# Softmax denominators on 64 rows per head, a division in quarters, and an earlier place for the first output tile

## The chip, the core and the metric

The kernel runs on one core of one Trainium2 chip. The metric is the device time of one execution in microseconds (us), lower is better. Of the core's engines, PE (TensorE) multiplies matrices, with PEld for its weight loads; DVE (VectorE), ACT (ScalarE) and POOL (GpSimd) work on elements; SP (SyncE) issues the DMAs.

## The reference

One inference step of a trunk of two layers, over 1024 latent tokens ("sample") and 128 context tokens ("prompt"), width 1024, all in fp32. Layer 0 joins grouped-query attention (mixer A, 8 heads of 64, 1152 keys for a latent token) with a pooling mixer B; layer 1 joins a neighbourhood attention (mixer C) with a latent attention (mixer D, 8 heads, keys of 96, values of 64). The change touches the softmax of A and D and the output projections behind them:

```python
def blocked_attention(q, k, v):
    ...
        s = jnp.einsum('bqkgd,bnkd->bkgqn', qblk, k, preferred_element_type=jnp.float32) * scale
        p = jax.nn.softmax(s, axis=-1).astype(v.dtype)
        return jnp.einsum('bkgqn,bnkd->bqkgd', p, v)
...
    y = jnp.concatenate([o_a * jax.nn.silu(ga), o_b * jax.nn.silu(gb)], axis=-1) @ w_out
```

## The kernel before, in words

The order of instructions on each engine is the order in which the Python code issues them; semaphores, put in by the framework, make an engine wait for its inputs and for free buffers. `weave(main, fill, frac)` (L27) spreads the steps of `fill` evenly over the first `frac` of the steps of `main`, by the costs written beside each step.

A and D each run as eight **units**, one for a pair of heads and half of the latent tokens (512). A unit goes over nine key tiles of 128 keys (`kt` 0 to 8, called the first to the ninth). For each key tile and head, PE makes scores `st` [128 keys, 512 queries] in PSUM, and ACT takes the exponential into `P` (or `Px`). For the denominator, POOL adds the `P` of the key tiles into `acc` [128, 2 heads, 512]; in the last unit of a mixer DVE does it. PE multiplies `P` with the values into one PSUM bank `pv`, which has 64 rows for each head, in the groups of key tiles of `PV_GROUPS`: 0 and 1 behind key tile 3, 2 and 3 behind 5, 4 to 6 behind 8, and 7 and 8 inside the next unit. Between these, the next unit's maxima are made as `fill`: 24 times PE forms a piece of scores `mp` [128 queries, 384 keys] and DVE reduces it (`mx`, L948), then `ms` (L953) joins them and PE turns them into a row (`mT`), which the next unit's scores subtract.

The **end of a unit** runs as a list `tail` within the next unit, one step per key tile: the last `pv`; nothing; gate times `pv` into `gT()` (a slice of `oT` in A, of `gd` in D); then `ColSums`. Its `sums` (fourth key tile) has PE sum `acc` over the keys with a matrix of ones, four matmuls of 32 rows by 256 queries, into a bank `sum`, and DVE takes half of the reciprocals. `split` (fifth) takes the other half and splits the result `srow` in two parts that PE can read without loss, `Rhl`: the high one by a cast on ACT, the low one by a subtraction on DVE. `spread` (seventh) has PE copy these rows to the 64 rows of each head (bank `rb`, four matmuls with the constant `oneh`), and DVE multiplies `gT()` with it. The context tokens' attention in A (`prompt_A`, woven into units 3 to 5 as `side` steps, with `mpp`, `msp`, `mTp`) uses `ColSums` as well; that of D makes its sums pair by pair (`dsum`), has ACT copy them to a tile `psum`, and normalises all of them in `prompt_norm` at the end.

PSUM has eight banks of [128, 512]: three for `st` (tag A), five taken in turn by everything else (tag B: `mp`, `pv`, `sum`, `rb`, `mT`, `ggp` and the rest).

Behind the units comes the output projection `outproj` (L1213). For each of nine token tiles it splits the branch outputs into two parts `ohl` (a cast on DVE, a subtraction on POOL), PE multiplies them with the weights `whi` and `wlo` (the split of `raw`, by ACT and POOL) into two banks `yps`, and `post` normalises. Its first steps, `pre` (the gate rows `ggp`, two loads, the splits of tile 0), are `fill` of the last unit, spread over the first 77% of its steps (after a placeholder of cost 18000 in layer 0, in `extra`). The last unit's own tail runs inside the first output tile.

Of the kernel before, what the change touches and what calls it, by code (L numbers as in the profile page):

```python
# [55 lines left out]
class Kern:  # L56
# [108 lines left out]
    def setup(self):  # L165
# [13 lines left out]
        self.oneh = self.K([128, 2, 128], F32R, name="oneh")  # L179

    def setup2(self):
        oh = self.W([128, 2, 128], name="oh0")
        self.dma(oh, self.I["k_oneh"])
        self.vcopy(self.oneh, oh)
        self.negid = self.K([128, 128], F32R, name="negid")
        self.vts(self.negid, self.ident, -1.0)
# [742 lines left out]
class Unit:  # L929
# [71 lines left out]

    def fin(self):

        kn = self.kn
        R = ColSums(kn)

        def f0():
            g = self.gT()
            kn.vtt(g, g, self.pv)
        return [(1, f0), (440, lambda: R.sums(lambda h, c: self.acc[:, h, 256 * c:256 * c + 256])), (1, R.split),  # L1010
                (1, lambda: None), (440, lambda: R.spread(self.gT()))]


class ColSums:


    def __init__(self, kn):
        self.kn = kn

    def sums(self, src):  # L1020
        kn = self.kn
        b = self.b = kn.B("sum")[:, 0:256]
        for h in range(2):
            for c in range(2):
                o = 64 * h + 32 * c
                kn.mm(b[o:o + 32], kn.ones, src(h, c))
        self.R = kn.T([128, 256], tag="srow", bufs=1)
        self.half(0)

    def half(self, i):  # L1030
        c = slice(128 * i, 128 * i + 128)
        self.kn.nc.vector.reciprocal(out=self.R[:, c], in_=self.b[:, c])  # L1032

    def split(self):
        kn = self.kn
        self.half(1)
        hl = self.hl = kn.T([128, 2, 256], F32R, tag="Rhl", bufs=1)
        kn.acopy(hl[:, 0], self.R)
        kn.vtt(hl[:, 1], self.R, f32(hl[:, 0]), ALU.subtract)

    def spread(self, g):

        kn, hl = self.kn, self.hl
        b = kn.B("rb")
        for c in range(2):
            for x in range(2):
                kn.mm(b[:, 256 * c:256 * c + 256], kn.oneh[:, c, :], hl[:, x], x == 0, x == 1)
        kn.vtt(g, g, b)
# [5 lines left out]
def run_units(kn, units, side, frac=0.77, extra=None, two=True, skip=()):  # L1054

    tail = []
    for i, u in enumerate(units):
# [9 lines left out]
        for kt in range(u.nkt):  # L1067
# [68 lines left out]
def prompt_A(kn, Qs, KHp, KLp, Vp):  # L1136

    nc = kn.nc
    X = {}
# [33 lines left out]
    def s5():  # L1173
        pv = kn.B("pvp")
        for p in range(4):
            for h in range(2):
                kv = p // 2
                kn.mm(pv[64 * h:64 * h + 64, 128 * p:128 * p + 128], Vp[:, 64 * kv:64 * kv + 64], X["P"][:, 2 * p + h])
        g = kn.oTp[:, 0:4, :]
        kn.vtt(g, g, v4(pv))  # L1180
        Pv = X["P"].rearrange("p (c i h) q -> p c h i q", c=2, h=2)
        X["R"] = ColSums(kn)
        X["R"].sums(lambda h, c: Pv[:, c, h])

    def s7():
        X["R"].spread(kn.oTp[:, 0:4, :].rearrange("p j q -> p (j q)"))
# [4 lines left out]
    return L + [(600, s5), (1, lambda: X["R"].split()), (440, s7)]  # L1191
# [73 lines left out]
def attention_A(kn, units, Qs, KHp, KLp, Vp):  # L1265
# [11 lines left out]
    at = [(3, kt) for kt in range(2, 9)] + [(4, 7), (4, 8), (5, 1)]  # L1277
# [23 lines left out]
    tail.insert(-1, (4000, lambda: None))  # L1301
# [17 lines left out]
    tail = tail[:-1] + [(4000, lambda: None), tail[-1], (2000, lambda: None)] + L.prompt_norm()  # L1319
    tail.insert(-1, (2000, lambda: None))  # L1320
# [416 lines left out]
class UnitD(Unit):  # L1737
# [17 lines left out]
    def fin(self):  # L1755
# [3 lines left out]
        return super().fin() + ([(1, put)] if self.p < 3 else [])  # L1759
# [19 lines left out]
class Latent:  # L1779
# [262 lines left out]
    def prompt(self, p):  # L2042
# [41 lines left out]
        def s4():  # L2084
            P, V = X["P"], X["V"]
            b = kn.B("dsum")
            for h in range(2):
                kn.mm(b[32 * h:32 * h + 32, 0:128], kn.ones, P[:, h])
            c = p // 2
            for h in range(2):  # L2090
                o = 64 * h + 32 * c
                kn.acopy(self.psum[o:o + 32, 128 * (p % 2):128 * (p % 2) + 128], b[32 * h:32 * h + 32, 0:128])
            pv = kn.B("dpvp")
            for h in range(2):
# [5 lines left out]
    def prompt_norm(self):  # L2100

        R = ColSums(self.kn)
        R.b = R.R = self.psum
        g = self.kn.oTp[:, 4:8, :].rearrange("p j q -> p (j q)")
        return [(1, lambda: R.half(0)), (1, R.split), (440, lambda: R.spread(g))]


def layer1_latent(kn, H, gd, st, tail, pre, oc):
# [76 lines left out]
    L.psum = kn.T([128, 256], tag="psum", bufs=1)  # L2185
# [116 lines left out]
```

## Time and profile before

| | |
|---|---|
| time, median of 3 runs | 1600.57 us (1600.37 to 1601.91) |
| the profiled execution's own time | 1600.49 us |
| its span | 1598.7 us |
| mean granted clock of PE | 0.98 |
| attention A, its eight units | 333 to 543 us |
| mixer D, its eight units | 1190 to 1490 us |
| output projections | from 542 us and from 1488 us |

The profile is of one execution. A row of a group reads: line, engine, operation, output<-inputs, form, count, then busy time and mean ns of one, then the idle time of the engine ahead of it and what ended most of it. PE matmuls overlap, so the distance between two starts is what one costs, not its duration. An fp32 matmul (`pv`, `sum`, `ggp`) counts as two instructions, one of two-part operands (`st`, `mp`, `rb`, `yps`) as one. The granted clock is the share of full speed that PE's throttle let through in a stretch.

### The profile page before, as it was taken

How to read it: one execution, taken by the hardware profiler on the slowest of the kernel's cores; microseconds unless marked ns; L12 is line 12 of the kernel's file. 1: busy time of each engine (PE TensorE's matmuls, PEld its weight loads, DVE VectorE, ACT ScalarE, POOL GpSimd, SP SyncE). 2: the span in 40 equal slices, each digit the busy share in tenths (PEclk: the TensorE clock that was granted, in tenths of full speed). 3: DMA queues.
4: the chain of work that ended last, by engine and by line, in shares of the span. 5: the costliest groups of instructions: out<-in, count | busy, mean ns of one | idle time of the engine just before them, and what ended most of it. 6: DMA issues, size and time to landing. Idle time of an engine off the chain costs nothing. (4 is left out here: it accounts for less than half of the span.)

```text
span 1598.7 us, 23592 instructions
## 1 busy us (share of the span) xinstructions
PE 1518.5 (95%) x9095; PEld 1238.9 (77%) x9095; DVE 793.5 (50%) x1776; ACT 649.4 (41%) x1379; POOL 625.0 (39%) x499
## 2 busy tenths in 40 slices
PE   7989999989899999899999999999999999899998
PEld 5978998945555588898989898999976656565786
DVE  4565233357575555534354443423574555546633
ACT  4332211255555323445454544444454434444311
POOL 1743212058669323641303103001256556556421
PEclk8989999999999999999999999999999999999999
DMA  9352104120001232410403130131000000013241
GB/s 343 91 195 81 40 27 145 45 100 14 1 14 40 66 106 80 87 39 15 98 16 75 39 75 24 36 100 58 1 18 21 14 27 15 21 42 117 97 147 53
DMA packets 114080, 104.81 MB, mean 66 GB/s; under 512 B 41776, under 2 KB 99952, under 8 KB 113968
## 3 DMA queue, kind: packets, MB, share of 16 engines
q1 hardware_dynamic: 113792, 103.23, 21.7%
q8 instruction: 72, 1.18, 0.3%
q14 instruction: 40, 0.33, 0.1%
q10 hardware_dynamic: 176, 0.07, 0.0%
HBM read 87.54 MB, written 15.75 MB: 65 GB/s over the span
## 5 line engine op out<-in xcount | busy, mean ns | idle before, releaser
L948 DVE TENSOR_REDUCE mx<-mp 128x1 f32<-128x384 f32 x384 | 189.1, 548 | 99.4 <-PE mp L97 98.0
L124 POOL TENSOR_TENSOR acc<-acc,P 128x1024 f32<-128x1024 f32 x84 | 199.7, 2378 | 75.0 <-ACT P L980 70.0
L980 ACT ACTIVATE P<-st 128x512 f32<-128x512 f32 x256 | 147.2, 598 | 149.1 <-PE st L97 144.1
L124 POOL TENSOR_TENSOR wlo<-raw,whi 128x1024 fp32r<-128x1024 f32 x36 | 87.5, 2433 | 266.5 <-ACT whi L113 153.2
L97 PE MATMUL yps<-whi,ohl 128*128 128x512 f32 x576 | 182.8, 393 | 0.3 <-POOL ohl L124 0.3
L97 PE MATMUL cg<-hT1h,whi 128*128 128x384 f32 x480 | 170.3, 355 | 1.9 <-DVE hf L133 1.2
L97 PE MATMUL cg<-hT1h,wlo 128*128 128x384 f32 x480 | 163.4, 341 | 1.9 <-POOL wlo L124 1.9
L97 PE MATMUL cg<-hT1l,whi 128*128 128x384 f32 x480 | 162.9, 339 | 0.0
L97 PEld LDWEIGHTS yps<-whi,ohl 128*128 128x128 f32 x576 | 108.1, 188 | 25.2 <-issue 2.4
L97 PE MATMUL yps<-wlo,ohl 128*128 128x512 f32 x288 | 112.2, 389 | 0.0
L97 PE MATMUL gate<-hTh,whi 128*128 128x384 f32 x288 | 98.1, 341 | 4.2 <-ACT whi L113 4.2
L97 PE MATMUL gate<-hTh,wlo 128*128 128x384 f32 x288 | 97.8, 340 | 1.3 <-DVE wlo L121 1.3
L97 PE MATMUL gate<-hTl,whi 128*128 128x384 f32 x288 | 97.5, 339 | 0.0
L97 PEld LDWEIGHTS cg<-hT1h,whi 128*128 128x128 f32 x480 | 91.3, 190 | 6.6 <-issue 3.3
L97 PEld LDWEIGHTS cg<-hT1h,wlo 128*128 128x128 f32 x480 | 91.2, 190 | 2.2 <-POOL wlo L124 2.2
L1547 ACT ACTIVATE cs<-cs,cnm 128x640 f32<-128x640 f32 (+1 forms) x64 | 54.8, 857 | 91.9 <-DVE cnm L131 90.9
L97 PEld LDWEIGHTS cg<-hT1l,whi 128*128 128x128 f32 x480 | 91.4, 190 | 0.4
L124 POOL TENSOR_TENSOR acc<-P 128x1024 f32<-128x1024 f32 x14 | 33.6, 2398 | 102.3 <-ACT P L980 101.7
L113 ACT CAST whi<-raw 128x1024 fp32r<-128x1024 f32 (+2 forms) x60 | 61.9, 1037 | 24.1 <-DMA raw<-in_w_in_e 11.0
L97 PE MATMUL pv<-P,dV 128*64 128x512 f32 x288 | 71.4, 622 | 0.2
L97 PE MATMUL st<-QP,KH 128*128 128x512 f32 x144 | 61.8, 429 | 6.6 <-ACT P L980 3.8
L97 PE MATMUL mp<-KH,QP 128*128 128x384 f32 x192 | 57.3, 357 | 6.8 <-DVE msp L1156 2.2
(417 smaller groups left out, 3561.5 us busy)
## 6 DMA issues: line engine op xcount, KB each, us to landing
raw<-in_w_in_o SPq DMA_DIRECT2D x20, 512.0 KB, 4.0
raw<-in_w_in_e SPq DMA_DIRECT2D x18, 512.0 KB, 7.2
wmb<-in_w_mod SPq DMA_DIRECT2D x16, 512.0 KB, 8.4
wm<-in_w_mod SPq DMA_DIRECT2D x16, 512.0 KB, 6.5
wg<-in_w_mod SPq DMA_DIRECT2D x16, 512.0 KB, 4.6
x<-xr SPq DMA_DIRECT2D x9, 512.0 KB, 2.8
xr<-x SPq DMA_DIRECT2D x9, 512.0 KB, 4.8
xn<-in_x_sample SPq DMA_DIRECT2D x8, 512.0 KB, 7.1
```

Source lines behind the costliest of these rows:

```text
L97: self.nc.tensor.matmul(out=out, lhsT=l, rhs=r, start=st, stop=sp)
L113: self.nc.scalar.copy(out=out, in_=in_)
L124: self.nc.gpsimd.tensor_tensor(out=out, in0=a, in1=b, op=op)
L948: kn.nc.vector.tensor_reduce(out=self.mx[:, h, t, c:c + 1], in_=b, axis=AX.X, op=ALU.max)
L980: kn.nc.scalar.activation(out=P[:, h], in_=a, func=AF.Exp, scale=self.scale)
L1547: nc.scalar.activation(out=s[:, 0:n], in_=s[:, 0:n], func=AF.Exp, bias=nm, accum_out=sm)
```

## The change

1. The sums take 64 rows per head: `ones` is [128, 64], and two matmuls of 64 rows by 512 queries fill the bank, each head's 64 rows all holding the same sums. They are issued right ahead of the group of `pv` at the fourth key tile.
2. `Rhl`, its cast and its subtraction, the spread (`rb`) and `oneh` are gone. `divide` takes the reciprocals in four quarters of 128 queries, one step of the tail each, and after the fourth multiplies `gT()` with `srow` [128, 512].
3. The context tokens follow: A's with `divide`, D's with sums, reciprocal and multiply for each pair; `psum` and `prompt_norm` are gone.
4. In the last unit `fill` is spread over all steps (1.0 for 0.77), so `pre` comes later. Its sums come fifth in the tail that runs within the first output tile (960 and 4000 are the costs of the sums and of a placeholder ahead of them).

```diff
-        self.ones = self.K([128, 32], name="ones")
+        self.ones = self.K([128, 64], name="ones")
...
+    def sums(self):
+        kn = self.kn
+        self.sb = kn.B("sum")
+        for h in range(2):
+            kn.mm(self.sb[64 * h:64 * h + 64, :], kn.ones, self.acc[:, h, :])
...
-        return [(1, f0), (440, lambda: R.sums(lambda h, c: self.acc[:, h, 256 * c:256 * c + 256])), (1, R.split),
-                (1, lambda: None), (440, lambda: R.spread(self.gT()))]
-class ColSums:
...
+        return [(1, f0)], divide(kn, lambda: self.sb, self.gT)
+def divide(kn, b, g):
+    box = {}
+    def part(i):
+        if i == 0:
+            box["r"] = kn.T([128, 512], tag="srow", bufs=1)
         c = slice(128 * i, 128 * i + 128)
+        kn.nc.vector.reciprocal(out=box["r"][:, c], in_=b()[:, c])
+        if i == 3:
+            kn.vtt(g(), g(), box["r"])
+    return [(1, lambda i=i: part(i)) for i in range(4)]
...
             if kt in PV_GROUPS:
                 ks = PV_GROUPS[kt]
+                if sums:
+                    main.append((1, sums))
+                    sums = None
                 main.append((1, lambda u=u, ks=ks: u.pvs(*ks)))
-        weave(main, fill, frac)
-        tail = [(1, lambda u=u: u.pvs(7, 8)), (1, lambda: None), *u.fin()]
-    return tail
+        weave(main, fill, frac if i + 1 < len(units) else 1.0)
+        a, b = u.fin()
+        sums = u.sums
+        tail = [(1, lambda u=u: u.pvs(7, 8)), (1, lambda: None), *a, (1, lambda: None), *b]
+    return tail[:3] + [(4000, lambda: None), (960, sums)] + tail[4:]
...
-    return L + [(600, s5), (1, lambda: X["R"].split()), (440, s7)]
+    return L + [(600, s5)] + divide(kn, lambda: X["s"], lambda: kn.oTp[:, 0:4, :].rearrange("p j q -> p (j q)"))
...
-            b = kn.B("dsum")
+            b = kn.B("dpv")
             for h in range(2):
-                kn.mm(b[32 * h:32 * h + 32, 0:128], kn.ones, P[:, h])
-            c = p // 2
+                kn.mm(b[64 * h:64 * h + 64, 0:128], kn.ones, P[:, h])
             for h in range(2):
-                o = 64 * h + 32 * c
-                kn.acopy(self.psum[o:o + 32, 128 * (p % 2):128 * (p % 2) + 128], b[32 * h:32 * h + 32, 0:128])
-            pv = kn.B("dpvp")
-            for h in range(2):
-                kn.mm(pv[64 * h:64 * h + 64, 0:128], V[:, 64 * h:64 * h + 64], P[:, h])
+                kn.mm(b[64 * h:64 * h + 64, 128:256], V[:, 64 * h:64 * h + 64], P[:, h])
             g = kn.oTp[:, 4 + p, :]
-            kn.vtt(g, g, pv[:, 0:128])
+            kn.vtt(g, g, b[:, 128:256])
+            r = kn.T([128, 128], tag="dr", bufs=1)
+            nc.vector.reciprocal(out=r, in_=b[:, 0:128])
+            kn.vtt(g, g, r)
```

How this moves the work is seen at three places. The first is DVE in A's second unit, which carries the end of the first. A row is a line, an operation, output<-inputs, the output's size and a count (`QP` is the query preparation of the unit after the next). Before:

```order
L948 TENSOR_REDUCE mx<-mp 128x1 x9
L121 TENSOR_TENSOR oT_2624<-oT_2624,pv 128x512
L948 TENSOR_REDUCE mx<-mp 128x1 x3
L1032 RECIPROCAL srow<-sum 128x128
L948 TENSOR_REDUCE mx<-mp 128x1 x2
L1032 RECIPROCAL srow<-sum 128x128
L121 TENSOR_TENSOR Rhl<-srow,Rhl 128x256
L948 TENSOR_REDUCE mx<-mp 128x1 x8
L121 TENSOR_TENSOR oT_2624<-oT_2624,rb 128x512
L948 TENSOR_REDUCE mx<-mp 128x1
L953 TENSOR_REDUCE ms<-mx 128x8
```

And of the change, from the same place:

```order
L944 TENSOR_REDUCE mx<-mp 128x1 x10
L121 TENSOR_TENSOR oT_2620<-oT_2620,pv 128x512
L944 TENSOR_REDUCE mx<-mp 128x1 x4
L1023 RECIPROCAL srow<-sum 128x128
L944 TENSOR_REDUCE mx<-mp 128x1 x5
L1023 RECIPROCAL srow<-sum 128x128
L944 TENSOR_REDUCE mx<-mp 128x1 x4
L1023 RECIPROCAL srow<-sum 128x128
L949 TENSOR_REDUCE ms<-mx 128x8
L1023 RECIPROCAL srow<-sum 128x128
L121 TENSOR_TENSOR oT_2620<-oT_2620,srow 128x512
```

Two reciprocals with the subtraction behind the second became four reciprocals, three of them among the maxima and the last behind `ms`, with the multiply behind it. The second place is PE in the same unit, from the fourth key tile on. Before:

```order
L97 MATMUL mp<-KH_893,QP 128x384
L97 MATMUL sum<-acc,ones 32x256 x4
L97 MATMUL mp<-KH_893,QP 128x384
L97 MATMUL pv<-P,V 64x512 x4
L97 MATMUL st<-QP,KH_893 128x512
```

And of the change:

```order
L97 MATMUL mp<-KH_889,QP 128x384
L97 MATMUL sum<-acc,ones 64x512 x2
L97 MATMUL pv<-P,V 64x512 x4
L97 MATMUL st<-QP,KH_889 128x512
L97 MATMUL st<-QM,KL_891 128x512
```

The sums stand next to `pv`, in its shape; the four matmuls of `rb`, three key tiles on, are gone. The third place is DVE at the end of layer 0's last unit, from the third reciprocal (before: the second) to the first output tile's casts. Before:

```order
L1032 RECIPROCAL srow<-sum 128x128
L121 TENSOR_TENSOR Rhl<-srow,Rhl 128x256
L121 TENSOR_TENSOR acc<-acc,Px 128x1024
L121 TENSOR_TENSOR acc<-acc,P 128x1024
L121 TENSOR_TENSOR oT_2867<-oT_2867,rb 128x512
L118 CAST ohl<-oT_1842 128x256
L118 CAST ohl<-oT_2276 128x256
L118 CAST ohl<-oT_2624 128x256
L118 CAST ohl<-oT_2867 128x256
L121 TENSOR_TENSOR acc<-acc,P 128x1024 x2
```

And of the change:

```order
L1023 RECIPROCAL srow<-sum 128x128
L121 TENSOR_TENSOR acc<-acc,P 128x1024
L1023 RECIPROCAL srow<-sum 128x128
L121 TENSOR_TENSOR oT_2863<-oT_2863,srow 128x512
L121 TENSOR_TENSOR acc<-acc,P 128x1024
L118 CAST ohl<-oT_1838 128x256
L118 CAST ohl<-oT_2272 128x256
L118 CAST ohl<-oT_2620 128x256
L118 CAST ohl<-oT_2863 128x256
```

The casts of the first output tile stood ahead of the unit's last two accumulations and now stand behind the last one; on PE `ggp` moved likewise, from ahead of the last four score steps to behind them.

More of the change, by code (lines that the diff above doesn't have):

```diff
@@ L1009, in f0 @@
             kn.vtt(g, g, self.pv)
-        return [(1, f0), (440, lambda: R.sums(lambda h, c: self.acc[:, h, 256 * c:256 * c + 256])), (1, R.split),
-                (1, lambda: None), (440, lambda: R.spread(self.gT()))]
-class ColSums:
[L1017 to L1022, printed above, removed]
-        for h in range(2):
-            for c in range(2):
-                o = 64 * h + 32 * c
[L1026 to L1030, printed above, removed]
-        c = slice(128 * i, 128 * i + 128)
[L1032 to L1048, printed above, removed]
+        return [(1, f0)], divide(kn, lambda: self.sb, self.gT)
[4 more added lines that the diff above has]
+            box["r"] = kn.T([128, 512], tag="srow", bufs=1)
+        c = slice(128 * i, 128 * i + 128)
+        kn.nc.vector.reciprocal(out=box["r"][:, c], in_=b()[:, c])
+        if i == 3:
+            kn.vtt(g(), g(), box["r"])
+    return [(1, lambda i=i: part(i)) for i in range(4)]
 PV_GROUPS = {3: (0, 1), 5: (2, 3), 8: (4, 5, 6)}
 def run_units(kn, units, side, frac=0.77, extra=None, two=True, skip=()):
-    tail = []
+    tail, sums = [], None
     for i, u in enumerate(units):
@@ L1178, in s5 @@
                 kn.mm(pv[64 * h:64 * h + 64, 128 * p:128 * p + 128], Vp[:, 64 * kv:64 * kv + 64], X["P"][:, 2 * p + h])
+        Pv = X["P"].rearrange("p (j h) q -> p j h q", h=2)
+        X["s"] = kn.B("sum")
+        for h in range(2):
+            kn.mm(v4(X["s"])[64 * h:64 * h + 64], kn.ones, Pv[:, :, h, :])
         g = kn.oTp[:, 0:4, :]
         kn.vtt(g, g, v4(pv))
[L1181 to L1186, printed above, removed]
     L = [(440, s1)]
@@ L1276, in attention_A @@
         side.setdefault((u, kt + 3), []).append((1, lambda i=i: wo.split1(i)))
-    at = [(3, kt) for kt in range(2, 9)] + [(4, 7), (4, 8), (5, 1)]
+    at = [(3, kt) for kt in range(2, 9)] + [(4, kt) for kt in (7, 8)] + [(5, kt) for kt in range(3)]
     for u, a in zip(at, L):
@@ L1758, in put @@
             self.kn.dma(self.L.oc[t, :, 4 + self.p, :].rearrange("t p q -> p t q"), self.gT().rearrange("p (t q) -> p t q", q=128))
-        return super().fin() + ([(1, put)] if self.p < 3 else [])
+        a, b = super().fin()
+        return a, b + ([(1, put)] if self.p < 3 else [])
     def mlhs(self, h, t):
@@ L2085, in s4 @@
             P, V = X["P"], X["V"]
-            b = kn.B("dsum")
+            b = kn.B("dpv")
             for h in range(2):
-                kn.mm(b[32 * h:32 * h + 32, 0:128], kn.ones, P[:, h])
-            c = p // 2
+                kn.mm(b[64 * h:64 * h + 64, 0:128], kn.ones, P[:, h])
             for h in range(2):
-                o = 64 * h + 32 * c
-                kn.acopy(self.psum[o:o + 32, 128 * (p % 2):128 * (p % 2) + 128], b[32 * h:32 * h + 32, 0:128])
-            pv = kn.B("dpvp")
-            for h in range(2):
-                kn.mm(pv[64 * h:64 * h + 64, 0:128], V[:, 64 * h:64 * h + 64], P[:, h])
+                kn.mm(b[64 * h:64 * h + 64, 128:256], V[:, 64 * h:64 * h + 64], P[:, h])
             g = kn.oTp[:, 4 + p, :]
-            kn.vtt(g, g, pv[:, 0:128])
+            kn.vtt(g, g, b[:, 128:256])
+            r = kn.T([128, 128], tag="dr", bufs=1)
+            nc.vector.reciprocal(out=r, in_=b[:, 0:128])
+            kn.vtt(g, g, r)
         return [(600, s0), (110, s1), (110, s2), (330, s3), (200, s4)]
[L2100 to L2105, printed above, removed]
 def layer1_latent(kn, H, gd, st, tail, pre, oc):
@@ L2184, in layer1_latent @@
     p6 = kn.open_tmp("t4")
-    L.psum = kn.T([128, 256], tag="psum", bufs=1)
     L.load_uk(1)
```

8 lines of the change are left out of this document (removed).

## The prediction

> **What bounds the kernel now.** I read the page first, then busy time by stretch, then the waits of PE in the two stretches that the change touches, and then the timeline around each of these waits.
>
> ```profile
> PE 1518.5 (95%) x9095; PEld 1238.9 (77%) x9095; DVE 793.5 (50%) x1776; ACT 649.4 (41%) x1379; POOL 625.0 (39%) x499
> ```
> ```profile
> 333.00:543.00 210.00, 198.20 (x974) 112.76 (x971) 136.01 (x228) 111.71 (x201) 151.46 (x66) 0.97 0.08 24
> 1190.00:1490.00 300.00, 284.10 (x1391) 185.07 (x1390) 162.60 (x281) 136.82 (x255) 182.38 (x97) 0.99 0.13 41
> ```
>
> The first line is busy time over the whole span. The next two are the eight units of attention A and the eight of mixer D (start:end, length, busy time of PE, PEld, DVE, ACT and POOL, granted clock, DMA share, GB/s). PE is busy for 95% of the span, so two things can move the end: less work on PE, or fewer waits of PE. In A, DVE is at 65% and POOL at 72%: an engine at that load can hold PE up wherever its work comes in clumps.
>
> The waits of PE, first in A and then in D (total us, times, longest):
>
> ```profile
> PE st L97 <- ACT P L980: 3.8, 3, 2.9
> PE st L97 <- ACT Px L980: 2.8, 1, 2.8
> PE mp L97 <- DVE msp L1156: 2.2, 1, 2.2
> PE mp L97 <- DVE mx L948: 1.6, 1, 1.6
> PE mp L97 <- DVE srow L1032: 0.7, 3, 0.3
> ```
> ```profile
> PE dsp L97 <- DVE dKl L121: 4.3, 2, 2.2
> PE mT L97 <- DVE ms L953: 2.0, 3, 0.7
> PE mp L97 <- DVE mx L948: 1.7, 4, 1.0
> PE mp L97 <- ACT psum L113: 1.3, 2, 0.6
> PE st L97 <- ACT P L980: 0.5, 1, 0.5
> ```
>
> A long wait costs more than itself. These four windows are those behind the wait for `msp`, the long one for `Px` and the two for `dKl`:
>
> ```profile
> 426.80:430.30 3.50, 3.50 (x10) 0.51 0.00 0
> 532.60:536.10 3.50, 3.50 (x12) 0.51 0.00 0
> 1280.00:1283.60 3.60, 3.60 (x9) 0.53 0.00 0
> 1365.40:1368.90 3.50, 3.50 (x12) 0.51 0.00 0
> ```
>
> PE is busy throughout, at a granted clock of 0.51 to 0.53. At half speed 3.5 us hold the work of 1.75, so each costs about 1.7 us on top of its wait.
>
> **The change part by part.** Term a is PE's own work. The chain of waits (start, us, group) prices a round of sums, two key tiles of `pv`, and a spread:
>
> ```profile
> 1470.51 0.57 PE sum L97 x8
> 1471.08 1.87 PE pv L97 x8
> ...
> 1480.23 0.48 PE rb L97 x4
> ```
>
> The new sums have the shape of one key tile of `pv` (two matmuls of 64 rows by 512), so I price them at half of 1.87, 0.93. A site costs 0.57 + 0.48 = 1.05 before and 0.93 after, −0.12. There are 17 (16 units, and the context tile of A): −2.0. The context tile of D loses a spread more, −0.5; its sums only change shape. Sums and `pv` now stand together, which saves a change of tile shape at each site; for that I take −0.4, under 0.03 each. **a = −2.9**; ends −1.5 and −4.
>
> Term b is the wait for `msp`, in the unit that carries the context tile. Its cause, on POOL, DVE and PE (start, us, group, idle time before and its releaser):
>
> ```profile
> 422.21 2.36 POOL L124 TENSOR_TENSOR acc<-acc,Px 128x1024 f32<-128x1024 f32 x1 [3.42 <-ACT Px L980]
> ```
> ```profile
> 422.39 2.46 DVE L121 TENSOR_TENSOR Rhl<-srow,Rhl 128x256 fp32r<-128x256 f32 x1 [2.76 <-ACT Rhl L113]
> ```
> ```profile
> 422.16 0.51 PE L97 MATMUL mp<-KH,QP 128*128 128x384 f32 x2
> 422.51 0.39 PE L97 MATMUL st<-QP,KH 128*128 128x512 f32 x1
> 422.74 0.39 PE L97 MATMUL st<-QM,KL 65*128 65x512 f32 x1
> 422.97 0.34 PE L97 MATMUL mp<-KH,QP 128*128 128x384 f32 x1
> 425.50 0.44 PE L97 MATMUL mp<-KH,QP 128*128 128x384 f32 x1 [2.20 <-DVE msp L1156]
> ```
>
> DVE waits 2.76 us for ACT's `Rhl` cast, then its subtraction drags for 2.46 beside POOL's accumulation, and the reductions that free PE's banks stand behind it. Cast and subtraction are both deleted. What is late next is one reciprocal, which never stretches, while the subtraction did (ns, shortest/median/longest):
>
> ```profile
> L1032 DVE RECIPROCAL srow<-sum x34: 894/948/955, 363.9 to 1493.6; 128x128 f32<-128x128 f32 x34
> L121 DVE TENSOR_TENSOR Rhl<-srow,Rhl x17: 424/1126/2620, 368.3 to 1495.0; 128x256 fp32r<-128x256 f32 x17
> ```
>
> So 2.2 goes, and the slow window with it: **b = −3.9**; ends −1.5 (another wait brings a window there) and −4.
>
> Term c is the end of layer 0's last unit. `st` waited there because ACT stood at an `Rhl` cast, which waited for the second reciprocal behind DVE's accumulations. That 2.8, 0.7 more of the waits for `P`, and a slow window of 1.7 go: 5.2. Against it, the first output tile's casts (DVE) and low halves (POOL) now stand behind the unit's last accumulation. Their prices:
>
> ```profile
> 532.37 1.23 DVE L121 TENSOR_TENSOR acc<-acc,Px 128x1024 f32<-128x1024 f32 x1 [0.56 <-ACT Px L980]
> ...
> 533.17 3.32 PE L97 MATMUL ggp<-ggrow,ident 128*128 128x256 f32 x8
> ...
> 537.01 1.05 ACT L113 CAST whi<-raw 128x1024 fp32r<-128x1024 f32 x1
> ```
>
> The same accumulation beside POOL's work:
>
> ```profile
> 539.08 3.03 DVE L121 TENSOR_TENSOR acc<-acc,P 128x1024 f32<-128x1024 f32 x1 [1.65 <-ACT P L980]
> ```
> ```profile
> L118 DVE CAST ohl<-oT x32: 230/289/837, 535.4 to 618.2; 128x256 fp32r<-128x256 f32 x32
> L124 POOL TENSOR_TENSOR ohl<-oT,ohl x32: 716/740/862, 535.8 to 620.3; 128x256 fp32r<-128x256 f32 x32
> ```
>
> From the fifth key tile on DVE has five accumulations of 1.23, four reciprocals of 0.95, a multiply of 0.7 and a cast of 0.3: 10.9 us, begun about 1.1 after PE begins that key tile. PE has five key tiles of scores (0.46 a pair, so 0.93 each: 4.7), `pv` of two key tiles (1.9), `ggp` (3.3 at half clock, so about 1.6) and `pv` of three more (2.8): 11.0, and some 1.0 of waiting where a weight cast now stands between two exponentials on ACT. So DVE ends as PE arrives, and what is left shows: 0.1 at the cast, 0.7 at POOL's first low half, and up to 1.8 if POOL slows an accumulation as at 539.08, of which I take 1.1. With the 1.0 that is 2.9, and another 1.0 for a slow window at odds of 6 in 10: 3.9. **c = −1.3**; ends −4 and +2.
>
> Term d: in D, `dsp` waited for `dKl` behind the `Rhl` pair, 2.15 twice, with a slow window each. `dKl` itself and the cast ahead of it stay, so I leave 1.7 of each wait (−0.9) and give each slow window one chance in four to go (a quarter of 3.4, −0.9): **d = −1.8**; ends 0 and −7.
>
> Term e: `mp` waited 1.3 for the copies into `psum`, which are gone, and 3.3 in A and D for maxima, some behind `Rhl`. I take all of the first and half of the second: **e = −3.0**; ends 0 and −4.6. Term f: the end of D, as c, but with three passes of scores per half key tile, 2.3 us more cover. Of c's waits 0.3 and 0.7 stay, and the 0.5 at `st` goes: **f = +0.5**; ends −0.5 and +3.
>
> Term h is the price. The sums' bank is now held from the fourth key tile to the fourth reciprocal, near the unit's end, where it came free after the second. With `pv`'s bank it leaves three of five to `mp`; three of the four reciprocals stand among the maxima, and the third ahead of `ms`, for which `mT` waits.
>
> ```profile
> L948 DVE TENSOR_REDUCE mx<-mp x384: 493/549/560, 303.0 to 1457.7; 128x1 f32<-128x384 f32 x192
> ```
>
> The 24 maxima of a unit are 2.67 per key tile: 2.67 × 0.5 + 0.95 = 2.3 us of DVE, against 0.93 of scores, 0.93 of `pv` and 2.67 × 0.17 of `mp` on PE, also 2.3. DVE doesn't fall behind for good, but where a reciprocal meets a clump of `mp`, PE waits up to 0.95. No row shows how often; the nearest, the 0.7 that `mp` waits for `srow` in A, is three waits of 0.2 to 0.3, and with one bank less I take one wait of 0.75 in each of seven units: **h = +5.2**; ends 0 and 7 × 3 × 0.95 = 20. In D a unit lasts 37.5 us with the same maxima, and I take nothing.
>
> Term i is one more wait that is long enough for a slow window: **i = +1.7**; ends 0 and +5. By the Trainium skill, "TensorE: Matmul & The Clock Gate", section "HAM oscillation — how this bites in real kernels", only idle gaps over about 3.4 us slow PE down. The windows above follow waits of 2.1 to 2.8, so the trace doesn't agree. By that rule i would be nothing, and the sum 1.7 lower.
>
> The profiled run took 1600.49 (span 1598.7 and 1.8 around it), 0.08 below the median of 1600.57. −2.9 − 3.9 − 1.3 − 1.8 − 3.0 + 0.5 + 5.2 + 1.7 = **−5.5: 1595.0**.
>
> **The rivals.** *The banks eat it* (25%): a reciprocal meets a clump twice per unit, so h is 10.4 and the sum −0.3: 1600.2. For it: DVE and PE are even in these key tiles. Against it: a reciprocal with a dragging `Rhl` behind it was a longer block, and `mp` waited only 1.6 for `mx` in all of A.
>
> *Slower through the banks* (13%): all three reciprocals hold PE for about 0.8, so h is 7 × 2.4 = 17, and two more slow windows come, 3.4; the sum is 9.7: 1610. It makes the kernel slower from the point where a unit loses over 2.0 us (h over 14). Milder versions lie near 1605.
>
> *The multiply drags* (10%). The last multiply read `rb` from PSUM and never dragged; now both operands lie in SBUF, as the subtraction's did, which went from 0.42 to 2.62:
>
> ```profile
> L121 DVE TENSOR_TENSOR oT<-oT,rb x8: 676/678/690, 373.6 to 555.0; 128x512 f32<-128x512 f32 x8
> ```
>
> If it takes 2.6 in 13 units, and two thirds of the extra 1.9 reach PE, that is 16 on the sum: 1611. Against it: it stands behind the last maximum, with three key tiles of `pv` (2.8) as cover. The Trainium skill, "GPSIMD Engine Reference", section "Specifications", says that GpSimd shares its SBUF interfaces with VectorE and contends with instructions of two SBUF inputs; the rows of `Rhl` agree. By it the multiply would drag wherever POOL works, which is this rival.
>
> *It doesn't do what it says*: no chance of its own. The deleted instructions are gone; only where PE waits instead is open.
>
> **How the numbers follow.** Forecast 52%, the rivals 25, 13 and 10. The forecast's own terms leave about 1588 to 1600. The range of 1588 to 1605 holds that, the first rival, and the milder versions of the slower ones. About 0.2%, 3.2 us, is what a measurement of this kernel tells from no change, so faster is below 1597.4 and slower above 1603.8. Faster: the forecast but for its upper end, 0.48. Slower: the last two rivals but for their mildest versions, 0.20. The rest is within: 0.32.
>
> **What would show it.** For a, a round of `sum` in the chain of waits at 0.93. For b and c, no wait of `mp` for `msp` and none of `st` for `Px`, and a granted clock of 1.0 after 426.8. For d, `dsp` behind `dKl` by less than 1.8 each. For h, the waits of `mp` in A for `mx` and `srow`, now 2.3, at 5 to 8; over 15 would be the slower rival. For the multiply, a median over 1.5 us, with `mp` or `qT` waiting for it. The forecast is wrong if over three new slow windows appear, or if `yps` waits over 4 us for `ohl` at either end.

## The result, and the profile after

The change makes the kernel slower: 1610.32 us, median of 4 runs (1607.43 to 1613.03), against 1601.24 of the kernel before in its 4 runs (1600.37 to 1603.26); the ratio is 1.006, 95% interval 1.0042 to 1.0078. The profiled execution took 1607.43 us, of which 1605.7 is its span. (The title calls the first output tile's place an earlier one; it is a later one, as point 4 of the change and its rows of instructions have it.)

Three lines of the page and of the clocks tell where the 7.0 us between the two spans are. Busy time by engine, of the changed kernel:

```profile
PE 1521.7 (95%) x8955; PEld 1234.6 (77%) x8955; DVE 822.5 (51%) x1796; ACT 642.1 (40%) x1353; POOL 627.7 (39%) x499
```

The span and the mean granted clock, first of the kernel before, then of the changed one:

```profile
core 0: 1598.7 us, clock 0.980
```
```profile
core 0: 1605.7 us, clock 0.976
```

PE idles for 1605.7 − 1521.7 = 84.0 us, before for 80.2: +3.8. Half speed takes (1 − 0.976) × 1605.7 = 38.5 us, before 32.0: +6.5. What is left, PE's work at full speed, falls from 1486.5 to 1483.2: −3.3. (Some idle time lies within slow windows; with only their busy part counted, the work is 1492.4 and 1489.0, 3.4 less.) So PE has less to do, as it was meant to, and loses three times as much in waits and in slow windows, the stretches of half speed behind them.

The waits of PE in A with its end, and in D with its end (total us, times, longest), of the changed kernel:

```profile
PE st L97 <- ACT P L976: 4.0, 4, 2.9
PE mp L97 <- DVE mx L944: 3.6, 8, 1.1
PE yps L97 <- DVE ohl L118: 3.3, 1, 3.3
PE sum L97 <- DVE oT L121: 0.5, 2, 0.4
PE mp L97 <- DVE oT L121: 0.2, 1, 0.2
```
```profile
PE mp L97 <- DVE dKl L121: 4.3, 4, 1.1
PE mp L97 <- DVE dr L2073: 4.2, 3, 1.6
PE mT L97 <- DVE ms L949: 3.8, 5, 2.0
PE yps L97 <- DVE ohl L118: 3.4, 1, 3.4
PE st L97 <- ACT QH L113: 1.7, 2, 0.9
```

Gone are the waits for `msp`, for `Px`, for `srow` and for `psum`. New are `yps` waiting for the first cast of the output at both ends, and in D `mp` for the context tokens' reciprocal `dr` and `QH`, with `mT` waiting longer. Gone as well is what was the largest wait in D before, not among the lines shown ahead of the result:

```profile
PE dq L97 <- POOL uql L124: 4.4, 3, 1.5
```

Three stretches of PE in the changed kernel (start:end, length, busy, granted clock, DMA share, GB/s): where the slow window behind the wait for `msp` was, and behind the two waits of `yps`:

```profile
426.80:430.30 3.50, 3.50 (x26) 1.00 0.00 0
536.10:543.00 6.90, 6.14 (x14) 0.51 0.05 10
1491.90:1498.80 6.90, 5.96 (x14) 0.51 0.03 13
```

Behind each of the two waits stand two windows of half speed in a row, 6.8 us, in which PE is busy for 6.1 and 6.0 and so loses some 3.0. That isn't a rule: in the fourth experiment below a wait of 3.4 was followed by one window, in the tenth one of 2.8 by two. Each end thus costs some 6.4 us, half of it behind the wait; at A's end the kernel before lost about 5.2 in its waits for `Px` and `P` and the window behind them.

The table is worked out from the starts of each unit's first exponential (`P<-st`), in the two profiled executions:

| unit | 1 | 2 | 3 | 4 | 5 | 6 | 7 |
|---|---|---|---|---|---|---|---|
| A before, us | 28.5 | 25.2 | 25.3 | 36.4 | 26.3 | 25.6 | 24.1 |
| A after | 28.5 | 25.2 | 25.3 | 32.7 | 26.7 | 27.7 | 24.2 |
| D before | 33.8 | 41.3 | 45.2 | 41.3 | 45.0 | 41.4 | 38.9 |
| D after | 36.2 | 39.0 | 47.6 | 39.0 | 50.1 | 39.1 | 39.3 |

Regular units of A are as long as before. The fourth, with the wait for `msp`, lost 3.7. The sixth, in which A's context tokens are divided, gained 2.1. In D the odd-numbered units, which carry the context tokens, are longer, and the even-numbered ones, behind them, shorter. Taken by pairs, the first two come out nearly even (75.1 before and 75.2 after, 86.5 and 86.6): what the odd unit takes longer, the next gives back, and the waits of `dq` that went are as large as those for `dr` that came. The third pair is 2.8 longer (86.4 and 89.2), and has 10.2 us of slow windows where there were 3.4. From the last unit's start to the first output tile's end A gained 1.6 and D 4.8.

Three places show what makes DVE late. At the end of D's first unit, DVE (start, us, engine, group), first before, then after:

```profile
1205.45 0.29 DVE L121 TENSOR_TENSOR oTp<-oTp,dpvp 128x128 f32<-128x128 f32 x1
1205.66 0.17 DVE L953 TENSOR_REDUCE ms<-mx 128x8 fp32r<-128x24 f32 x1
1205.75 0.32 DVE L118 COPY uqr<-uqr 128x96 f32<-128x96 f32 x2
```
```profile
1204.09 0.29 DVE L121 TENSOR_TENSOR oTp<-oTp,dpv 128x128 f32<-128x128 f32 x1
1204.29 0.95 DVE L2073 RECIPROCAL dr<-dpv 128x128 f32<-128x128 f32 x1
1205.28 1.62 DVE L121 TENSOR_TENSOR oTp<-oTp,dr 128x128 f32<-128x128 f32 x1
1206.82 0.17 DVE L949 TENSOR_REDUCE ms<-mx 128x8 fp32r<-128x24 f32 x1
1206.91 2.46 DVE L118 COPY uqr<-uqr 128x96 f32<-128x96 f32 x2
```

and POOL beside it, after:

```profile
1204.40 4.79 POOL L124 TENSOR_TENSOR acc<-acc,P 128x1024 f32<-128x1024 f32 x2 [1.19 <-ACT P L976]
```

The multiply by `dr` ends at 1206.90, 0.15 us behind the first of POOL's two accumulations (2.35 us from 1204.40), and the two copies end at 1209.4, 0.2 behind the second. Before, the copies ran 0.12 us ahead of POOL's start and took 0.32. The reciprocal of 0.95 was enough to push everything behind it into POOL's time. PE's `mT` waits 2.0 for `ms`, and ACT's cast of `uqr`, behind which stand `QH` and the next unit's scores, is late as well.

The second place is the end of D's last unit, on DVE, with POOL beside it:

```profile
1484.93 2.51 DVE L121 TENSOR_TENSOR acc<-acc,P 128x1024 f32<-128x1024 f32 x1
...
1488.35 2.88 DVE L121 TENSOR_TENSOR gd<-gd,srow 128x512 f32<-128x512 f32 x1
1491.15 1.21 DVE L121 TENSOR_TENSOR acc<-acc,P 128x1024 f32<-128x1024 f32 x1
1492.28 0.35 DVE L118 CAST ohl<-ocs 128x384 fp32r<-128x384 f32 x1
```

```profile
1483.51 2.86 POOL L124 TENSOR_TENSOR wlo<-raw,whi 128x1024 fp32r<-128x1024 f32 x1 [2.39 <-ACT whi L113]
1488.33 2.35 POOL L124 TENSOR_TENSOR wlo<-raw,whi 128x1024 fp32r<-128x1024 f32 x1 [1.97 <-DVE srow L1023]
```

POOL splits weights here. The accumulation, which needs 1.23, takes 2.51 and ends 1.1 behind POOL's first split; the multiply, which needs 0.69, takes 2.88 and ends 0.55 behind the second. The last accumulation and the cast stand behind it, and `yps` starts at 1492.78.

The third place is the end of A's last unit: DVE, then ACT's last exponentials, then PE's first scores of the fifth key tile and its wait:

```profile
520.13 3.41 DVE L121 TENSOR_TENSOR acc<-acc,P 128x1024 f32<-128x1024 f32 x1
...
525.38 1.23 DVE L121 TENSOR_TENSOR acc<-acc,Px 128x1024 f32<-128x1024 f32 x1
...
536.43 2.91 DVE L118 CAST ohl<-oT 128x256 fp32r<-128x256 f32 x6
```
```profile
527.68 2.08 ACT L976 ACTIVATE P<-st 128x512 f32<-128x512 f32 x4
```
```profile
521.00 0.50 PE L97 MATMUL st<-QP,KH 128*128 128x512 f32 x1
...
536.86 0.77 PE L97 MATMUL yps<-whi,ohl 128*128 128x512 f32 x1 [3.32 <-DVE ohl L118]
```

DVE goes from one instruction to the next without a pause from 520.13 to the cast. The last exponential ends at 529.76, 5.5 us before the last accumulation starts at 535.29: the cast waits for DVE's own row, not for PE or ACT. DVE comes to the fifth key tile's accumulation, at 525.38, 4.4 us after PE began that key tile, behind an accumulation of 3.41 beside POOL.

Durations over the kernel (ns, shortest/median/longest):

```profile
L121 DVE TENSOR_TENSOR oT<-oT,srow x8: 691/1504/2177, 373.2 to 554.8; 128x512 f32<-128x512 f32 x8
L121 DVE TENSOR_TENSOR gd<-gd,srow x8: 691/1176/2876, 1247.4 to 1510.8; 128x512 f32<-128x512 f32 x8
L121 DVE TENSOR_TENSOR oTp<-oTp,srow x1: 2693/2693/2693, 472.3 to 472.3; 128x512 f32<-128x512 f32 x1
```

### The profile page after: what moved, and what is told of

Its sections match the earlier page's. It is cut to its first block, busy times and chain, and to the rows that moved or that the text cites. A ratio compares the mean times of both kernels' runs of the same rounds, so it can differ in the third digit from the quotient of the medians.

```text
span 1605.7 us, 23306 instructions
## 1 busy us (share of the span) xinstructions
PE 1521.7 (95%) x8955; PEld 1234.6 (77%) x8955; DVE 822.5 (51%) x1796; ACT 642.1 (40%) x1353; POOL 627.7 (39%) x499
## 5 line engine op out<-in xcount | busy, mean ns | idle before, releaser
L124 POOL TENSOR_TENSOR acc<-acc,P 128x1024 f32<-128x1024 f32 x84 | 203.0, 2417 | 69.7 <-ACT P L976 65.7
L1023 DVE RECIPROCAL srow<-sum 128x128 f32<-128x128 f32 x68 | 63.5, 943 | 14.7 <-PE sum L97 14.5
L430 ACT ACTIVATE y<-yps 128x512 f32<-128x512 f32 x34 | 20.2, 597 | 121.7 <-PE yps L97 117.4
```

The lines of the kernel that those rows point to most:

```text
L124: self.nc.gpsimd.tensor_tensor(out=out, in0=a, in1=b, op=op)
L430: nc.scalar.activation(out=y[:, n], in_=box["a"][n], func=AF.Square, accum_out=box["s2"][:, n:n + 1])
L1023: kn.nc.vector.reciprocal(out=box["r"][:, c], in_=b()[:, c])
```

## The experiments

The theories: **1**, the first output tile is prepared too late; **2**, the new DVE instructions, those of two SBUF operands above all, hold up what stands behind them. Each time is a median, with the ratio to the kernel before and its 95% interval. The ratio is to runs of that kernel taken beside the experiment's, whose median was 1600.97 in the first four, 1602.45 in the next three, 1602.97 in the eighth and ninth and 1602.80 in the last two; so across these groups the ratios compare better than the medians. The expectations count units from 0: their even units of D are the odd-numbered ones here.

**First: the tile at its old place.**

```diff
-        weave(main, fill, frac if i + 1 < len(units) else 1.0)
+        weave(main, fill, frac)
...
+        if i + 2 == len(units):
+            b = [(1, lambda q=b[2 * k:2 * k + 2]: [f() for _, f in q]) for k in range(2)] + b[4:]
```

> The changed kernel, but in the last unit of A and of D the first output tile is prepared at its old place (the fill over 0.77 and 0.85 of the steps), and the unit's tail takes two quarters of the division per key tile, so that the division still stands ahead of the tile's casts. Theory 1, the late first tile: in the changed kernel yps waits 3.3 and 3.4 us for the cast at the two ends and two half-speed windows of 6.8 us follow (3.4 lost in each). Both waits and both windows go, and the time falls by 8 to 12 us, to about that of before. Rival, the division of the context tokens in D is what costs: the ends only change their kind of wait, and the time falls by 0 to 3 us.

1597.6 us (10 runs), ratio 0.9986 (0.9974 to 0.9997): 12.7 below the changed kernel, a little beyond the range of theory 1. (The old place is 0.77 of the steps in A, 0.85 in D.) From the last unit's start to the first output tile's end it is 5.7 us shorter than the changed kernel in A and 5.6 in D. The waits at D's end are now

```profile
PE yps L97 <- POOL ohl L124: 0.5, 1, 0.5
PE yps L97 <- DVE ohl L118: 0.2, 1, 0.2
```

and at A's end 0.3 for POOL. The late tile costs more than the whole loss. (The second part of the diff, alone, is the seventh experiment.)

**Second: the late place alone, in the kernel before.**

```diff
-        weave(main, fill, frac)
+        weave(main, fill, frac if i + 1 < len(units) else 1.0)
```

> The kernel before, with one edit of the change alone: in the last unit the fill is spread over all of the steps. Theory 1 in its plain form, the place alone costs: 5 to 9 us slower than before, with waits of yps for the cast of about 3 us at both ends. Rival: the place costs only because four reciprocals and the multiply stand in DVE's row between the last accumulations; with the old division, which is through by the seventh key tile, yps waits for less than 1.5 us at each end, and the time is within 3 us of before.

1604.27 us (10 runs), ratio 1.0027 (1.0009 to 1.0045): between the two. A's end has no wait for the cast, D's end has one of 3.1 and a slow window. In the kernel before, the place costs a fourth to a third of what it costs in the changed one. At A's end PE comes late itself there: it still waits 2.8 for `Px`, with a slow window, which gives DVE the time that it needs.

**Third: D's context tokens multiply from PSUM.**

```diff
-            r = kn.T([128, 128], tag="dr", bufs=1)
-            nc.vector.reciprocal(out=r, in_=b[:, 0:128])
-            kn.vtt(g, g, r)
+            nc.vector.reciprocal(out=b[:, 256:384], in_=b[:, 0:128])
+            kn.vtt(g, g, b[:, 256:384])
```

> The changed kernel, but D's context tokens take their reciprocals into PSUM (the free half of the same bank), so that the multiply by them reads one operand from PSUM. Theory 2, the multiply of two SBUF operands is held up beside POOL's accumulation (291 to 2037 ns in the changed kernel): it falls to about 300 ns in all four, mT waits 0.5 to 1.0 us in D's first unit in place of 2.0, and the time falls by 2 to 4 us. Rival, the reciprocal of 0.95 us itself, at this place in DVE's row, is what is waited for: under 1.5 us of gain.

1611.0 us (4 runs), ratio 1.0057 (1.0037 to 1.0078): no gain. D's first unit is 1.5 us shorter (34.7), as theory 2 had it, its multiplies take at most 0.29 us, and `mT` waits at most 0.8; but `mp` now waits 5.6 for the bank, up to 2.0 at a time, since the bank is given back after the multiply.

**Fourth: no division of D's context tokens.**

```diff
-            r = kn.T([128, 128], tag="dr", bufs=1)
-            nc.vector.reciprocal(out=r, in_=b[:, 0:128])
-            kn.vtt(g, g, r)
```

> The changed kernel without the reciprocal and the second multiply of D's context tokens: their outputs stay undivided. Theory 2, the context division costs D's even units their time: the waits of mp for dr (4.2 us in three) and most of those of mT for ms go, the units 0, 2 and 4 of D are 2 to 4 us shorter each, and the time falls by 5 to 9 us. Rival, these waits only took the place of others that come back: the time falls by less than 3 us.

1606.87 us (5 runs), ratio 1.0039 (1.0024 to 1.0054): 3.5 below the changed kernel, between the theories. The first unit is back at 33.7, but the units behind are longer again (40.4 for 39.0), and 27.3 us of slow windows lie between 1180 and 1510.

**Fifth: the units' last multiply reads PSUM.**

```diff
-            box["r"] = kn.T([128, 512], tag="srow", bufs=1)
...
-        kn.nc.vector.reciprocal(out=box["r"][:, c], in_=b()[:, c])
+        kn.nc.vector.reciprocal(out=b()[:, c], in_=b()[:, c])
...
-            kn.vtt(g(), g(), box["r"])
+            kn.vtt(g(), g(), b())
```

> The changed kernel, but the units and A's context tokens take their reciprocals in place in the PSUM bank of the sums, so that the last multiply reads one operand from PSUM. Theory 2, this multiply is held up beside POOL (691 to 2876 ns in the changed kernel, 2693 for A's context tokens) and PE pays for it: all seventeen multiplies take about 690 ns, the sixth unit of A is 1.5 us shorter, yps waits about 1.2 us in place of 3.4 at D's end, and the time falls by 3 to 6 us. Rival: where POOL works, the accumulation behind the multiply is held up in its place, and the bank is held 0.7 us longer; the time is within 2 us of the changed kernel's.

1603.72 us (10 runs), ratio 1.0009 (0.9996 to 1.0021): 6.6 below the changed kernel, more than either. But the places were not those foreseen: A's sixth unit is no shorter than in the changed kernel (27.8 for 27.7), so that what lengthens it isn't the multiply and stays open, and `yps` still waits 2.9 and 2.8 at the ends. At D's end the last accumulation is held up in the multiply's place (2.75 us); at A's end the multiply wasn't held up in the changed kernel either (0.69). The profiled execution was the slowest of the ten, 1608.59, so that it doesn't show the gain; the ninth experiment does.

**Sixth: the tile early, and D's context divided one unit later.** Over the first experiment:

```diff
-            r = kn.T([128, 128], tag="dr", bufs=1)
-            nc.vector.reciprocal(out=r, in_=b[:, 0:128])
-            kn.vtt(g, g, r)
+            X["r"] = kn.T([128, 128], tag="dr", bufs=1)
+            kn.acopy(X["r"], b[:, 0:128])
+        def s5():
+            g = kn.oTp[:, 4 + p, :]
+            nc.vector.reciprocal(out=X["r"], in_=X["r"])
+            kn.vtt(g, g, X["r"])
...
-            side.setdefault((2 * p, 2 + i), []).append(a)
+            side.setdefault((2 * p, 2 + i) if i < 5 else (2 * p + 1, 2), []).append(a)
```

> The first output tile at its old place as in the first experiment, and D's context tokens divided later: ACT copies their sums out of PSUM at once, and the reciprocal and the multiply stand in the next unit, at its third key tile. If the two causes (the late tile, worth 12.7 us of median in the first experiment, and the context division, worth 3.5 in the fourth) are of different places, they add: 1593 to 1596, 5 to 8 us faster than before. Rival: the two share their half-speed windows, or the copy on ACT costs what the division did: 1597 to 1599, no better than the first experiment.

1605.46 us (12 runs), ratio 1.0024 (1.0013 to 1.0036): worse than either theory, and 7.9 above the first experiment. The waits in D say why:

```profile
PE mp L97 <- DVE mx L944: 6.3, 4, 1.8
```

The division now stands among the next unit's maxima and holds them up there, in the even-numbered units, which are 3.6 to 5.4 us longer; its multiply, 0.29 us by itself, takes 0.92 to 1.92 beside POOL.

**Seventh: the late place with an early division** (the second part of the first experiment's diff alone):

```diff
+        if i + 2 == len(units):
+            b = [(1, lambda q=b[2 * k:2 * k + 2]: [f() for _, f in q]) for k in range(2)] + b[4:]
```

> The changed kernel with the first output tile at its new, late place, but with two quarters of the division per key tile in the last unit, so that DVE is through with it two key tiles earlier. Theory 1a, the queue: the four reciprocals and the multiply between the last accumulations make the cast late; yps then waits under 1.5 us at A's end and at D's, and the time falls by 6 to 10 us. Theory 1b, the place: what the cast waits for is the last accumulation, whatever stands ahead of it; yps waits about 3 us at both ends still, and the time falls by 0 to 2 us. In the second experiment (the old division at the late place) A's end had no such wait and D's end one of 3.1, so that one end may follow each.

1611.93 us (4 runs), ratio 1.0061 (1.0041 to 1.0081): no gain. `yps` waits 4.3 at A's end and 3.2 at D's. Theory 1b: the cast stands behind the last accumulation, and with the division earlier the sum of DVE's work ahead of it is the same. It isn't an exponential that is waited for: at A's end the last one ends at 529.8, and DVE, busy without a pause, starts the last three accumulations at 533.7, behind one that took 3.13 beside POOL.

**Eighth: the tile early, D's context divided at the very end.** Over the first experiment:

```diff
-            r = kn.T([128, 128], tag="dr", bufs=1)
-            nc.vector.reciprocal(out=r, in_=b[:, 0:128])
-            kn.vtt(g, g, r)
+            kn.acopy(self.psum[:, 128 * p:128 * p + 128], b[:, 0:128])
...
+    def prompt_norm(self):
+        kn = self.kn
+        def part(i):
+            c = self.psum[:, 128 * i:128 * i + 128]
+            kn.nc.vector.reciprocal(out=c, in_=c)
+            if i == 3:
+                g = kn.oTp[:, 4:8, :].rearrange("p j q -> p (j q)")
+                kn.vtt(g, g, self.psum)
...
-    for _, f in run(wo, {0: tail}):
+    for _, f in run(wo, {0: tail, 1: L.prompt_norm()}):
```

> The first output tile at its old place as in the first experiment, and D's context tokens divided at the very end: ACT copies each pair's sums out of PSUM, and four reciprocals and one multiply stand within the second output tile, where DVE has little to do. Theory 2 in the form that the sixth experiment left (the reciprocal of a pair costs wherever it stands among the maxima of a unit: there mp waited 6.3 us for maxima): the waits for dr and most of mT's for ms go and none take their place but 1 to 2 us for the copies, the half-speed time between 1180 and 1510 falls from 20.5 to 7 to 14 us, and the time is 1590 to 1595. Rival: what brings the half-speed windows in D's third and fifth unit are the waits for dKl, which stay: the time is 1596 to 1599, that of the first experiment.

1595.64 us (6 runs), ratio 0.9954 (0.9938 to 0.9970): between the two. The slow windows between 1180 and 1510 fell to 17.1 only, not to 7 to 14, and those in D's third and fifth unit stayed, as the rival had it; that the waits for `dKl` bring them isn't shown. The waits for `dr` and most of those for `ms` are gone, but another came to the front:

```profile
PE st L97 <- ACT QH L113: 4.5, 3, 2.5
```

These are the units behind a context unit, which start late: `QH` waits on ACT behind the cast of `uqr`, whose copies on DVE stand behind the units' own multiply, as in the third unit:

```profile
1286.56 1.83 DVE L121 TENSOR_TENSOR gd<-gd,srow 128x512 f32<-128x512 f32 x1
1288.31 2.47 DVE L118 COPY uqr<-uqr 128x96 f32<-128x96 f32 x2
```

**Ninth: the eighth with the fifth.** Over the eighth:

```diff
-        kn.nc.vector.reciprocal(out=box["r"][:, c], in_=b()[:, c])
+        kn.nc.vector.reciprocal(out=b()[:, c], in_=b()[:, c])
...
-            kn.vtt(g(), g(), box["r"])
+            kn.vtt(g(), g(), b())
```

> As the one before it, and the units take their reciprocals in place in PSUM, as in the fifth experiment. Theory: the fifth experiment's 6.6 us of median came from the last units, where the multiply stood ahead of the first output tile's cast; with the tile at its old place little is left of it: within 2 us of the one before it. Rival: the gain is in the regular units too, since every multiply of two SBUF operands held up something: 3 to 6 us faster than the one before it.

**1588.24 us** (6 runs, 1586.58 to 1592.07), ratio 0.9913 (0.9896 to 0.9929): faster than both kernels, and 7.4 below the eighth (6.6 by the ratios): the rival holds, and its range was too low. The wait of `st` for `QH` is gone from the table, and the multiplies no longer stretch:

```profile
L1021 DVE RECIPROCAL sum<-sum x68: 953/956/967, 364.0 to 1494.1; 128x128 f32<-128x128 f32 x68
L121 DVE TENSOR_TENSOR oT<-oT,sum x8: 686/688/689, 372.9 to 549.1; 128x512 f32<-128x512 f32 x8
L121 DVE TENSOR_TENSOR gd<-gd,sum x8: 686/686/690, 1241.2 to 1495.1; 128x512 f32<-128x512 f32 x8
```

Who waited for the copies of `uqr` (us, times): ACT's cast `uqh`, in the changed kernel and here (before, 4.2 in three):

```profile
  ACT uqh L113: 11.3, 4
```
```profile
  ACT uqh L113: 2.8, 2
```

**Tenth and eleventh: from the ninth, one part of the change put back.** In the tenth the `weave` line and the tail are the changed kernel's; in the eleventh D's context tokens are divided as there.

```diff
-        weave(main, fill, frac)
+        weave(main, fill, frac if i + 1 < len(units) else 1.0)
...
-        if i + 2 == len(units):
-            b = [(1, lambda q=b[2 * k:2 * k + 2]: [f() for _, f in q]) for k in range(2)] + b[4:]
```

> The ninth experiment with one part of the change put back: the first output tile at its late place, with four quarters one to a key tile. If the late place costs by itself, as the first experiment said, yps waits 2.5 to 3 us for the cast at each end with one or two half-speed windows each: 8 to 12 us more than the ninth experiment's 1588.2. Rival: the late place cost because the last multiply dragged ahead of the cast (2.9 us at D's end); with that multiply read from PSUM it costs under 5 us.

1601.47 us (10 runs), ratio 0.9995 (0.9982 to 1.0008): 13.2 above the ninth, a little beyond the range. `yps` waits 2.9 and 2.8 at the ends. The late place costs by itself; reading PSUM shortens its waits by only 0.4 and 0.6.

The eleventh, over the ninth:

```diff
-    for _, f in run(wo, {0: tail, 1: L.prompt_norm()}):
+    for _, f in run(wo, {0: tail}):
...
-            kn.acopy(self.psum[:, 128 * p:128 * p + 128], b[:, 0:128])
+            r = kn.T([128, 128], tag="dr", bufs=1)
+            nc.vector.reciprocal(out=r, in_=b[:, 0:128])
+            kn.vtt(g, g, r)
```

> The ninth experiment with another part of the change put back: D's context tokens divided pair by pair, with a reciprocal and a multiply of two SBUF operands in each even unit. If the division of a pair holds up maxima, ms and the copies behind it, mp waits 4 us for dr and mT 2 us for ms in the first unit, and the time is 3 to 8 us above the ninth experiment's. Rival: these are hidden by other waits at the units' ends, as the fourth experiment's odd units suggested: within 2 us.

1594.02 us (7 runs), ratio 0.9941 (0.9920 to 0.9961): 5.8 above the ninth, with `mp` waiting 4.3 for `dr` and `mT` 3.9 for `ms`; D's seventh unit takes 39.3 us, as in the changed kernel, for 37.5 in the ninth. Its interval touches the ninth's, so that of the three sizes this one is the least certain.

So, one part at a time from the best version: the late tile +13.2, the multiply from SBUF +7.4 (eighth), the division by pairs +5.8, in sum 26.4, against 22.1 for all three, the changed kernel. By the ratios the sum is 24.2 against 23.5, so the parts add up within the noise. Each part can be read from three pairs of versions that differ in it alone (differences of the ratios, times 1601 us):

| part | pairs | us |
|---|---|---|
| the late tile | changed and first; fifth and eleventh; tenth and ninth | 11.8; 10.9; 13.1 |
| the multiply from SBUF | changed and fifth; first and eleventh; eighth and ninth | 8.2; 7.2; 6.6 |
| D's division by pairs | first and eighth; fifth and tenth; eleventh and ninth | 5.1; 2.2; 4.5 |

By the intervals of the ratios, each of these is uncertain by some 3 to 4 us: the first two parts are clear of noise in every pair, the third in two of three, narrowly.

## Why the prediction was wrong

It forecast 1595.0 and a range up to 1605, and the time is 1610.3. Taken by its steps:

- **a, PE's work (−2.9): right.** −3.3 by the balance of the two profiles. From its start to that of `pv` a round of sums costs 0.91 in D's last unit (below), 0.88 to 1.01 in all of them at full speed, where the price was 0.93. What the saved change of tile shape is worth by itself no run shows.

```profile
1472.59 1.08 PE L97 MATMUL sum<-acc,ones 128*64 128x512 f32 x4
1473.50 1.89 PE L97 MATMUL pv<-P,dV 128*64 128x512 f32 x8
```

- **b, the wait for `msp` (−3.9): right.** The unit is 3.7 shorter, and the clock behind 426.8 is 1.00.
- **c and f, the ends of the last units (−1.3 and +0.5): wrong, and the main error.** The profiled executions show +1.6 and +4.8, and the late tile is worth 12.7 (first) to 13.2 (tenth). The step that failed is the sum for DVE: 10.9 us, begun 1.1 us after PE begins the fifth key tile, so that DVE ends as PE arrives and 0.1 shows at the cast; 3.3 and 3.4 showed. At A's end it was the start that was wrong. DVE began 4.4 us after PE and took 11.3 up to the end of the first cast, and PE arrived after 12.5, for 12.0 in the sum. The trace before had the same lag, 4.5 us:

```profile
524.43 0.50 PE L97 MATMUL st<-QP,KH 128*128 128x512 f32 x1
```
```profile
528.89 1.16 DVE L121 TENSOR_TENSOR acc<-acc,Px 128x1024 f32<-128x1024 f32 x1
```

At D's end it was DVE's work. It began 2.3 us after PE, and took 15.0: accumulations of 2.53 and 2.51 and the multiply of 2.88 each lost some 1.3 to 2.2 beside POOL's weight splits, for which the step had one allowance of 1.1, although the row at 539.08 was in the prediction; PE's 14.1 was as forecast (14.3). And it gave the slow windows as one of 1.7 at odds of 6 in 10; there were two in a row at each end, with some 3.0 lost.
- **D's context tokens ("its sums only change shape"): wrong by omission.** No term had the four reciprocals and four multiplies within the units, in place of two reciprocals and a spread at the end of the program. The experiments give them 2.2 to 5.1 by the ratios. The trace has new waits of 4.2 for `dr`, but in place of 4.4 that `dq` waited for `uql`, and by pairs of units only the slow windows are left of it.
- **d (−1.8): wrong.** The waits for `dKl` were 4.3 in two and are 4.3 in four, with 1.1 more at `sum`. `dsp` no longer waits, `mp` does.
- **e, `mp`'s waits for copies and maxima (−3.0): somewhat too large.** The 1.3 for `psum` went, and in D (1190 to 1490) the waits of `mp` for `mx` and `srow` fell from 2.1 to none, but in A they rose from 2.3 to 3.6: −2.1 in sum.
- **h, three banks for `mp` (+5.2): too large.** A's second and third unit have the same length to 0.1 us: PE's idle time rose in each by 0.35 us, about what the sums saved there, where h took 0.75. The first two rivals fall with it; that the second named 1610 and the third 1611, next to the measured 1610.3, is luck.
- **i, one more slow window (+1.7): too small.** Sorted by kind, the sum has −2.9 of PE's work, −1.0 of its idle time and −1.6 of half speed (b −1.7, c −0.7, d −0.9, i +1.7); the balance of the profiles has −3.3, +3.8 and +6.5. Of the 12.5 us between the forecast's −5.5 and the profile's +7.0, 8.1 are slow windows and 4.8 are waits; PE's work gives 0.4 back. Of the two signs that the prediction named for being wrong, one came, more than three new slow windows; the other, a wait of `yps` over 4 us, did not.
- **The third rival, the dragging multiply (10%): its mechanism was there,** with medians of 1176 and 1504 ns. Its path wasn't: it named the maxima and three key tiles of `pv` as cover, and the cost came by the copies of `uqr`, ACT and `QH`, and at D's end. The Trainium skill, "GPSIMD Engine Reference", section "Specifications", has GpSimd and VectorE contend where a VectorE instruction has two SBUF inputs or runs in a two-port mode; the trace agrees for the multiplies, and the copies of `uqr` (196 to 2354 ns), which have one SBUF input, are held up in the same way; whether they run in such a mode no run here shows.

What stays open: the changed kernel's D has 20.5 us of slow windows between 1180 and 1510, the kernel before 6.8, and the ninth 13.7. Which of several short waits close together brings such a window differs between executions: up to D's last unit the changed kernel, the first and the seventh experiment have the same code, and 13.7, 20.5 and 23.9 us of slow windows from 1180 on, in one profiled execution each. So the single windows in D's third and fifth unit aren't settled. The fifth experiment's gain is of the size that the same edit has elsewhere (8.2 by the ratios, for 7.2 and 6.6); where in the kernel it arose no profile shows.

## What to carry to other kernels

Removing work from the bounding engine pays only if the helper engine that takes it over isn't on the way of something else: price not the new instruction alone but what it pushes back, up to the next engine's big block of work. Before moving preparation of the next stage behind the end of the last, add up the helper's chain from the time at which the helper really gets there, which the trace before shows, with its slow durations, not its shortest, and with what a long wait brings behind it. Where two engines contend for SBUF, leaving the result in the PSUM bank in which it arose can free an instruction from that, if the bank can be spared: in the third experiment it could not, and PE waited 5.6 us for it.

## What the runs showed of the hardware

A DVE instruction with all of its operands in SBUF that starts while one of POOL runs isn't slowed, it waits. In the changed kernel eleven multiplies of 128x512 (0.69 us alone) took 0.75 to 2.88, and each ended 0.55 us behind POOL's instruction, an accumulation or a weight split; the five accumulations of 128x1024 (1.23 alone) that met a split took 2.51 to 3.41 and ended 1.08 behind it. So what such an instruction loses is what is left of POOL's 2.4 us when it starts: 0.20 us of copying took up to 2.35. One that started first kept its 0.69, and POOL's instruction took 2.8 in place of 2.4. The same multiply with one operand in PSUM took 686 to 690 ns in all seventeen places, and a reciprocal written back to PSUM 956 ns in place of 948.

The slow windows depend on the execution: up to attention's first exponential, where the programs hardly differ, the profiled execution of the changed kernel took 322.7 us, that of the third experiment, with the same code, 325.5. The kernel before ranged from 1597.5 to 1606.9 us over all runs of the study, as much as the change's whole effect. Only medians of several runs told the versions apart.
